# Spreading rotary tables, rotary key and row scales over partitions by DMA, and splitting the first weights of z one stage earlier

## The chip, the core and the metric

The kernel runs on one core of one Trainium2 chip. The metric is the device time of one execution in microseconds; a kernel's time is the median of its runs. TensorE does the matrix products, VectorE, ScalarE and GpSimd (POOL in the profile) the elementwise work, and DMAs are issued from the queues of SyncE (SP) and POOL.

## What is computed

One layer of an encoder: multi-head latent attention with a gate, then a gated embedding, on 1024 tokens of 1024 features in float32. The part that the change touches is the input side of the attention:

```python
h = rmsnorm(x, norm_g)
u = h @ w_in
c_q, c_kv, k_rope, z = split(u, [384, 640, 672])      # widths 384, 256, 32, 1024
q = (rmsnorm(c_q, q_norm) @ w_q_b)                    # 16 heads of 64 + 32
q_rope = apply_rope(q[..., 64:], cos, sin)
kv = (rmsnorm(c_kv, kv_norm) @ w_kv_b)                # 16 heads of 64 + 64
k_rope = apply_rope(k_rope, cos, sin)                 # one rotary key for all heads
...                                                   # scores, block-causal mask, softmax, values: o
y = (o * silu(z)) @ w_out
x = x + y
out = rmsnorm(x + sigmoid(rmsnorm(x) @ ple_gate) * (p @ ple_proj), final_norm)
```

## The kernel before

Every matrix product is made from float32 operands that are split into a high and a low part (`_hi`/`_lo`, `zh`/`zl`), and is the sum of three matmuls: hi*hi, hi*lo, lo*hi. A high part is a rounded copy, usually by ScalarE; the low part is the difference, usually by VectorE.

The stages on TensorE, one after the other, are: c_q, c_kv and the rotary key's input (`u_tile`, L203, eight tiles of 128 tokens, to 68.7 us); z (L487 to L509, eight products of 128 features by 1024 tokens, to 172 us); the projections of the first heads; then 16 heads of attention; then the output projection, the gate and the last norm.

In z each product c takes two half-products n = 2c and 2c + 1, of four 128x128 weight blocks each: 24 matmuls of 128x512 per half. `z_weights(n)` (L472) loads the half's weights to the staging tile `zs`, and splits them by four instructions on ScalarE (`zh`, L481) and four on VectorE (`zl`, L482). It is called one half-product ahead; there are three staging tiles and two pairs `zh`, `zl`, so a split waits until the half-product before last has been multiplied. These tiles lie where the weights of c_q, c_kv were, so no `zh`, `zl` can be written before that stage's last matmul. After a product VectorE multiplies it by `rbc`, the tokens' norm factors on all partitions (L498), which frees its PSUM tile (there are two, `ps_big`), and ScalarE makes the SiLU (L499).

Three things lie by token (token on the partition) and are needed by feature (token along the row): the norm factors `rx`, of which `rbc` has the same row on all 128 partitions; the rotary tables `cosT`, `sinT`, which become `cs`; and the rotary key `kr`, which becomes `kt` and then, split, half of `k_hi`, `k_lo` (L444 to L447). For each of them VectorE transposes 32x32 blocks and then places the blocks by 16 copies of 32 partitions each: `spread` (L449) for `rbc` and the two tables, `rope_key` (L426) for the key. `rope_key` stands in the text after product 1, the tables after product 2, the loads and casts of the first heads' weights (`weights(0)`, POOL, L381) after product 3, and the first rotary projections (`project_r`, which multiplies by `cs` and writes to DRAM from POOL's queue, L421) after products 4 and 5. Their scratch is two tiles of 4 KB per partition, `rt_tile` and `rh_tile`, of which there is one each.

The order of the text is not the order on an engine: the tile framework lists the instructions of each engine by its own estimate of when they are ready, the earlier text first among ready ones. On the chip each engine then runs its list strictly in order, and waits where an instruction's inputs are not there; DMA issues stand in the list of the engine whose queue they use.

Of the kernel before, what the change touches and what calls it, by code (L numbers as in the profile page):

```python
# [9 lines left out]
F32 = mybir.dt.float32  # L10
F32R = mybir.dt.float32r
BF16 = mybir.dt.bfloat16
I32 = mybir.dt.int32
AF = mybir.ActivationFunctionType
ALU = mybir.AluOpType
AX = mybir.AxisListType

P = 128
S = 1024
D = 1024  # L20
NT = S // P
KT = D // P
# [3 lines left out]
NOPE = 64  # L26
ROPE = 32
# [7 lines left out]
HF = ROPE // 2  # L35
# [16 lines left out]
def mla_ple_kernel(ctx, tc, x, x_t, p_t, pos, norm_g, w_c, w_z, q_norm, w_q, w_r, kv_norm, w_k, w_v,  # L52
# [6 lines left out]
    nc = tc.nc  # L59
    V, A, G = nc.vector, nc.scalar, nc.gpsimd  # L60
# [9 lines left out]
    def ps_tr():  # L70
        return psum.tile([P, 512], F32, tag="one", name="ps_tr", bufs=4)
# [8 lines left out]
    ident = const.tile([P, P], F32, name="ident")  # L80
# [4 lines left out]
    cosT = const.tile([P, NT, HF], F32, name="cosT")  # L85
    sinT = const.tile([P, NT, HF], F32, name="sinT")
    krw = const.tile([P, NT, ROPE], F32, name="krw")
    small = ctx.enter_context(pool("small", bufs=4))
# [4 lines left out]
    def rsqrt(v, n, name="rs_y", bufs=None):  # L93

        half = small.tile([P, n], I32, tag=f"rs_i{n}", name="rs_i", bufs=2)
        V.tensor_scalar(out=half, in0=v.bitcast(I32), scalar1=1, scalar2=None,  # L96
                        op0=ALU.logical_shift_right)
        y = small.tile([P, n], F32, tag=f"{name}{n}", name=name, bufs=bufs)
        V.tensor_scalar(out=y.bitcast(I32), in0=half, scalar1=-1, scalar2=0x5F3759DF,
                        op0=ALU.mult, op1=ALU.add)  # L100
        t = small.tile([P, n], F32, tag=f"rs_t{n}", name="rs_t", bufs=2)
        if n == 1:
            h = small.tile([P, 1], F32, tag="rs_h", name="rs_h", bufs=2)
            V.tensor_scalar(out=h, in0=v, scalar1=-0.5, scalar2=None, op0=ALU.mult)
            for _ in range(3):
                V.tensor_scalar(out=t, in0=y, scalar1=y, scalar2=h, op0=ALU.mult, op1=ALU.mult)  # L106
                V.scalar_tensor_tensor(out=y, in0=t, scalar=1.5, in1=y, op0=ALU.add, op1=ALU.mult)  # L107
            return y
        for _ in range(3):
            V.scalar_tensor_tensor(out=t, in0=y, scalar=-0.5, in1=y, op0=ALU.mult, op1=ALU.mult)  # L110
            V.tensor_tensor(out=t, in0=t, in1=v, op=ALU.mult)
            V.scalar_tensor_tensor(out=y, in0=t, scalar=1.5, in1=y, op0=ALU.add, op1=ALU.mult)
        return y
# [23 lines left out]
    def rt_tile(name):  # L137
        return both.tile([P, S], F32, tag="rt", name=name, bufs=1)

    def rh_tile(name):  # L140
        return both.tile([P, S], F32R, tag="rh", name=name, bufs=1)
# [4 lines left out]
    zT = zT_pool.tile([P, KT, S], F32, name="zT")  # L146
# [119 lines left out]
    def angles():  # L266
# [77 lines left out]
        V.scalar_tensor_tensor(out=cosT, in0=f, scalar=-2.0, in1=f, op0=ALU.mult, op1=ALU.mult)  # L344
        ts1(cosT, cosT, 1.0, ALU.add)

    pend = []
    for t in range(NT):
        un = u_tile(t)
        if t + 2 < NT:  # L350
            if t + 3 < NT:
                load_xT(t + 3)
            load_x(t + 2)
            stat_x(t + 2)
        if len(pend) == 2:
            u_transposes(*pend.pop(0))
        pend.append((t, un))
        if t == 4:
            angles()
        if t == NT - 2:  # L360
            mse = small.tile([P, NT], F32, name="mse", bufs=1)
            V.tensor_scalar(out=mse, in0=msx, scalar1=EPS, scalar2=None, op0=ALU.add)
            rx = rsqrt(mse, NT, name="rx", bufs=1)
    for t in range(NT):
        V.tensor_scalar(out=krw[:, t, :], in0=krw[:, t, :], scalar1=rx[:, t:t + 1], scalar2=None,
                        op0=ALU.mult)
# [40 lines left out]
    def project_r(g, hf):  # L407
# [12 lines left out]
        for z, d in zip((hi, lo), rq_of[g]):  # L420
            nc.gpsimd.dma_start(out=d.rearrange("c p n -> p c n")[:, :, cols], in_=z.bitcast(F32))  # L421

    def rope_key():  # L426
        kr = att1.tile([P, 512], F32, tag="ws", name="kr", bufs=2).rearrange("p (t n) -> p t n", t=NT)
        ra = small.tile([P, NT, HF], F32, name="ra", bufs=1)
        x1, x2 = krw[:, :, :HF], krw[:, :, HF:]
        k1, k2 = kr[:, :, :HF], kr[:, :, HF:ROPE]  # L430
        for dst, a, b, op in ((k1, cosT, sinT, ALU.subtract), (k2, sinT, cosT, ALU.add)):
            V.tensor_tensor(out=ra, in0=x2, in1=b, op=ALU.mult)
            V.tensor_tensor(out=dst, in0=x1, in1=a, op=ALU.mult)
            V.tensor_tensor(out=dst, in0=dst, in1=ra, op=op)
        V.tensor_copy(out=kr[:, :, ROPE:ROPE + HF], in_=k2)
        V.tensor_scalar(out=kr[:, :, ROPE + HF:], in0=k1, scalar1=-1.0, scalar2=None, op0=ALU.mult)
        blk, kt = rt_tile("kb"), rh_tile("kt").bitcast(F32)
        V.transpose(out=blk[:, :512], in_=kr.rearrange("p t n -> p (t n)"))
        b = blk[:, :512].rearrange("p (t f n) -> p f t n", t=NT, f=2)
        d = kt.rearrange("p (t q n) -> p q t n", q=4, n=32)  # L440
        for i in range(4):
            for j in range(4):
                V.tensor_copy(out=d[i * 32:(i + 1) * 32, j], in_=b[j * 32:(j + 1) * 32, i % 2])
        for e in range(2):  # L444
            rows = slice(NOPE * (1 - e), NOPE * (2 - e))
            A.copy(out=k_hi[e][rows], in_=kt[rows])
            sub_hi(V, k_lo[e][rows], kt[rows], k_hi[e][rows])  # L447

    def spread(src, dst, n):  # L449

        t, blk = rt_tile("spread"), rh_tile("blk").bitcast(F32)
        t, blk = (z[:, :NT * 32].rearrange("p (t n) -> p t n", t=NT) for z in (t, blk))
        V.tensor_copy(out=t.rearrange("p t (m n) -> p t m n", n=n) if n > 1 else t,
                      in_=src.unsqueeze(2).broadcast_to([P, NT, 32 // n, n]) if n > 1 else src.broadcast_to([P, NT, 32]))
        V.transpose(out=blk.rearrange("p t n -> p (t n)"), in_=t.rearrange("p t n -> p (t n)"))
        d = dst.rearrange("p (t q n) -> p q t n", q=4, n=32)
        for i in range(4):
            for j in range(4):
                V.tensor_copy(out=d[i * 32:(i + 1) * 32, j], in_=blk[j * 32:(j + 1) * 32])

    def rope_tables():
        for tab, src in zip(cs, (cosT, sinT)):
            spread(src, tab, HF)

    zph = ExitStack()

    zr = zph.enter_context(pool("zr", reuse_waits="tile"))
    rbc = zr.tile([P, S], F32, name="rbc")
    spread(rx.unsqueeze(2), rbc, 1)
    zw = zph.enter_context(pool("zw", reuse_waits="tile"))  # L470

    def z_weights(n):  # L472

        c, k0 = n // 2, n % 2 * 4
        stg, hi, lo = (zw.tile([P, 512], d, tag="z" + z, name="z" + z, bufs=m)
                       for z, d, m in (("s", F32, 3), ("h", F32R, 2), ("l", F32R, 2)))
        stg, hi, lo = (z.rearrange("p (k n) -> p k n", k=4) for z in (stg, hi, lo))
        nc.sync.dma_start(out=stg, in_=w_z[c].rearrange("p (k n) -> p k n", k=KT)[:, k0:k0 + 4, :])
        for k in range(4):
            g = g_col[:, k0 + k:k0 + k + 1]  # L480
            A.activation(out=hi[:, k, :], in_=stg[:, k, :], func=AF.Copy, scale=g)  # L481
            V.scalar_tensor_tensor(out=lo[:, k, :], in0=stg[:, k, :], scalar=g,  # L482
                                   in1=hi[:, k, :].bitcast(F32), op0=ALU.mult, op1=ALU.subtract)
        return hi, lo

    wz_next = z_weights(0)
    for c in range(KT):  # L487
        ps = ps_big()
        for k in range(KT):
            if k % 4 == 0:  # L490
                wz, n = wz_next, 2 * c + k // 4 + 1
                wz_next = z_weights(n) if n < 2 * KT else None
            for a, b in pairs:
                for hf in range(2):
                    nc.tensor.matmul(ps[:, hf * 512:(hf + 1) * 512], wz[b][:, k % 4, :],  # L495
                                     (hT_hi, hT_lo)[a][:, k, hf * 512:(hf + 1) * 512],
                                     start=k == 0 and a + b == 0, stop=k == KT - 1 and a == 1)
        V.tensor_tensor(out=zT[:, c, :], in0=ps, in1=rbc, op=ALU.mult)  # L498
        A.activation(out=zT[:, c, :], in_=zT[:, c, :], func=AF.Silu)  # L499
        if c < 2:  # L500
            u_transposes(*pend.pop(0))
        if c == 1:
            rope_key()
        if c == 2:
            rope_tables()
        if c == 3:
            weights(0)
        if c in (4, 5):
            project_r(0, c - 4)  # L509
# [157 lines left out]
    for n in range(len(blocks) + LAGV):  # L667
        if n < len(blocks):
            h, i = blocks[n]
# [208 lines left out]
```

## Time and profile before

| what | value |
|---|---|
| median of 3 runs | 728.67 us (726.36 to 729.4) |
| the profiled execution | 730.98 us |
| its span on the core | 729.2 us |
| TensorE busy | 708.6 us (97%) |
| VectorE busy | 547.4 us (75%) |
| ScalarE busy | 400.5 us (55%) |
| POOL busy | 198.8 us (27%) |

Matmuls are pipelined and their ends are modelled, so TensorE's busy share says only where it had something to do. Lost time in a stage is read from the starts of its matmuls, from the idle times and from the granted clock (1.00 is 2.4 GHz).

### The profile page before, as it was taken

Reading aid. Unit: us, or ns where it says so; the run is one execution under the profiler, and the core shown is the slowest. Engines: PE = TensorE matmul, PEld = TensorE weight load, DVE = VectorE, ACT = ScalarE, POOL = GpSimd, SP = SyncE. Lnnn points to the kernel's source line nnn. Section 1 sums busy time; section 2 is a strip of 40 time slices with the busy share of each in tenths; the row PEclk is TensorE's granted clock in tenths of the full one; section 3 lists DMA queues with packets and bytes.
Section 4 is the critical chain, followed back from the end, with each engine's and each line's share of the span. In section 5 each row is a group of like instructions: output and inputs, shape, how many; then the busy total and the mean of one; then the engine's idle time right before and its main releaser. Section 6 shows DMA issues by size and latency. Waiting matters only on the chain. (4 is left out here: it accounts for less than half of the span.)

```text
span 729.2 us, 11583 instructions
## 1 busy us (share of the span) xinstructions
PE 708.6 (97%) x4031; PEld 614.8 (84%) x4031; DVE 547.4 (75%) x1364; ACT 400.5 (55%) x919; POOL 198.8 (27%) x208
## 2 busy tenths in 40 slices
PE   9999989999999999999999999998999999999995
PEld 6998768888988999888999899887878887888884
DVE  6897894333988988888888888899654259798754
ACT  5743243334777786777768777776543144333322
POOL 0000300222225533453345532166146142000000
PEclk9999999999999999999999999999999999999998
DMA  8820311223102413034120431033474021111101
GB/s 305 286 86 1 105 40 48 79 95 95 51 16 82 141 30 88 15 106 129 45 75 0 152 99 45 16 113 91 136 283 130 1 82 35 44 36 37 58 29 58
DMA packets 25674, 61.32 MB, mean 84 GB/s; under 512 B 4112, under 2 KB 8080, under 8 KB 25616
## 3 DMA queue, kind: packets, MB, share of 16 engines
q1 hardware_dynamic: 23168, 52.19, 22.7%
q0 software_dynamic: 2304, 8.39, 3.1%
q8 instruction: 32, 0.52, 0.3%
q14 instruction: 26, 0.21, 0.1%
q10 hardware_dynamic: 144, 0.00, 0.0%
HBM read 47.92 MB, written 12.65 MB: 83 GB/s over the span
## 5 line engine op out<-in xcount | busy, mean ns | idle before, releaser
L733 PE MATMUL ps_big<-w,aTh 128*128 128x512 f32 (+1 forms) x480 | 139.1, 390 | 0.4 <-ACT sg L809 0.4
L733 PEld LDWEIGHTS ps_big<-w,aTh 128*128 128x128 f32 x480 | 89.4, 188 | 20.9 <-ACT sg L809 0.8
L601 ACT ACTIVATE prob<-ps_big,mx 128x384 f32<-128x384 f32 (+6 forms) x112 | 89.4, 799 | 16.3 <-DVE mx L596 15.7
L596 DVE TENSOR_REDUCE mx<-ps_big 128x1 f32<-128x384 f32 (+6 forms) x112 | 91.6, 817 | 1.8
L121 PE MATMUL ps_tr<-ident,prob 128*128 128x128 f32 x576 | 84.1, 273 | 1.9 <-ACT prob L601 1.9
L733 PE MATMUL ps_big<-w,aTl 128*128 128x512 f32 (+1 forms) x240 | 84.5, 390 | 0.1
L121 PEld LDWEIGHTS ps_tr<-ident,prob 128*128 128x128 f32 x576 | 68.3, 140 | 11.6 <-ACT prob L601 2.8
L91 DVE TENSOR_TENSOR pt8l<-ps_tr,pt8h 128x512 fp32r<-128x512 f32 (+3 forms) x128 | 71.0, 581 | 4.5 <-ACT pt8h L632 3.8
L591 PE MATMUL ps_big<-k_hi,qh 128*128 128x512 f32 (+2 forms) x176 | 67.7, 385 | 0.9 <-ACT prob L601 0.8
L649 POOL TENSOR_TENSOR zT<-o,zT 64x256 f32<-64x256 f32 x56 | 41.0, 734 | 94.8 <-DVE o L647 81.2
L632 ACT CAST pt8h<-ps_tr 128x512 fp32r<-128x512 f32 (+3 forms) x128 | 60.8, 509 | 4.7 <-PE ps_tr L121 4.3
L591 PE MATMUL ps_big<-k_lo,qh 128*128 128x512 f32 (+2 forms) x176 | 61.9, 352 | 0.0
L591 PE MATMUL ps_big<-k_hi,ql 128*128 128x512 f32 (+2 forms) x176 | 61.4, 349 | 0.0
L643 PE MATMUL ps_o<-pt8h,vals 128*128 128x256 f32 x224 | 57.6, 294 | 0.0
L643 PE MATMUL ps_o<-pt8l,vals 128*128 128x256 f32 x224 | 55.0, 282 | 0.0
L733 PEld LDWEIGHTS ps_big<-w,aTl 128*128 128x128 f32 x240 | 45.0, 188 | 10.2 <-POOL aTl L91 0.5
L495 PE MATMUL ps_big<-hT_hi,zh 128*128 128x512 f32 x128 | 41.3, 405 | 2.6 <-ACT zh L481 2.6
L481 ACT ACTIVATE zh<-zs,g_col 128x128 fp32r<-128x128 f32 x64 | 20.5, 397 | 42.4 <-PE ps_big L495 34.1
L495 PE MATMUL ps_big<-hT_hi,zl 128*128 128x512 f32 x128 | 40.7, 400 | 3.2 <-DVE zl L482 3.1
L116 ACT ACTIVATE jk<-xs 128x512 bf16<-128x512 f32 (+2 forms) x25 | 18.8, 750 | 44.9 <-DVE xs L811 37.0
L643 PEld LDWEIGHTS ps_o<-pt8l,vals 128*128 128x128 f32 x224 | 42.9, 191 | 0.0
L643 PEld LDWEIGHTS ps_o<-pt8h,vals 128*128 128x128 f32 x224 | 42.6, 190 | 0.0
(269 smaller groups left out, 1728.7 us busy)
## 6 DMA issues: line engine op xcount, KB each, us to landing
zT<-in_x SPq DMA_DIRECT2D x8, 512.0 KB, 4.8
zs<-in_w_z SPq DMA_DIRECT2D x16, 256.0 KB, 2.7
rlb<-rl SPq DMA_DIRECT2D x32, 128.0 KB, 3.1
wst<-in_w_out SPq DMA_DIRECT2D x8, 512.0 KB, 4.4
xs<-in_x SPq DMA_DIRECT2D x8, 512.0 KB, 7.4
wst<-in_ple_gate SPq DMA_DIRECT2D x8, 512.0 KB, 4.2
out<-xs SPq DMA_DIRECT2D x16, 256.0 KB, 2.0
zT<-in_x_t SPq DMA_DIRECT2D x6, 512.0 KB, 3.9
```

What stands on the lines that cost most here:

```text
L91: eng.tensor_tensor(out=lo, in0=src, in1=hi.bitcast(F32), op=ALU.subtract)
L116: A.activation(out=junk, in_=src, func=AF.Square, scale=n ** -0.5, accum_out=dst)
L121: nc.tensor.transpose(dst[:, j * P:(j + 1) * P], src[:, j * P:(j + 1) * P], ident)
L481: A.activation(out=hi[:, k, :], in_=stg[:, k, :], func=AF.Copy, scale=g)
L495: nc.tensor.matmul(ps[:, hf * 512:(hf + 1) * 512], wz[b][:, k % 4, :], (hT_hi, hT_lo)[a][:, k, hf * 512:(hf + 1) * 512], start=k == 0 and ...
L591: nc.tensor.matmul(ps[:, off + s0:off + s1], q[a][:, qs], (k_hi, k_lo)[b][e][:, s0:s1], start=a + b == 0, stop=a == 1)
L596: V.tensor_reduce(out=mx, in_=s, axis=AX.X, op=ALU.max, negate=True)
L601: A.activation(out=pr[:, :n], in_=s, func=AF.Exp, bias=mx, scale=1.0, accum_out=l)
L632: A.copy(out=hi[:, j0:j0 + n, half], in_=src)
L643: nc.tensor.matmul(ps[:, :256], w, z[:, j, :], start=j + n == 0, stop=j == last and n == 1)
L649: (V if h >= H - 2 else G).tensor_tensor(out=z, in0=o[top], in1=z, op=ALU.mult)
L733: nc.tensor.matmul(o, st[a][:, k, :], w[k][b][:, cols], start=k == 0 and a + b == 0, stop=k == nk - 1 and a == 1)
```

## The change

`rbc` is now made from a TensorE transpose of `rx`, written as a row of 4 KB to DRAM and read back to all 128 partitions by one DMA (`token_scales`). For the tables and the key, `token_rows` keeps VectorE's blockwise transposition, writes the blocks to a DRAM tile with one row per feature (four DMAs of 32 partitions for each 32 features, in runs of 128 bytes), and the rows are read back once for each place where they are needed: two reads for the key, four for each table. All these DMAs are issued from POOL's queue. The 16 copies of each are gone.

`z_weights` is moved ahead of the stage c_q, c_kv and called for half-products 0 and 1 in that stage's tile 6. These two are staged in `zT[:, 1, :]` and split into `rh_tile` and `rt_tile`. From then on weights are asked for two half-products ahead, with three pairs `zh`, `zl` and one staging tile.

```diff
@@ -344,6 +344,24 @@
         V.scalar_tensor_tensor(out=cosT, in0=f, scalar=-2.0, in1=f, op0=ALU.mult, op1=ALU.mult)
         ts1(cosT, cosT, 1.0, ALU.add)
 
+    def z_weights(n):
+
+        c, k0 = n // 2, n % 2 * 4
+        if n < 2:
+            cols = slice(n * 512, n * 512 + 512)
+            stg, hi, lo = (z[:, cols] for z in (zT[:, 1, :], *z_first))
+        else:
+            stg, hi, lo = (zw.tile([P, 512], d, tag="z" + z, name="z" + z, bufs=m)
+                           for z, d, m in (("s", F32, 1), ("h", F32R, 3), ("l", F32R, 3)))
+        stg, hi, lo = (z.rearrange("p (k n) -> p k n", k=4) for z in (stg, hi, lo))
+        nc.sync.dma_start(out=stg, in_=w_z[c].rearrange("p (k n) -> p k n", k=KT)[:, k0:k0 + 4, :])
+        for k in range(4):
+            g = g_col[:, k0 + k:k0 + k + 1]
+            A.activation(out=hi[:, k, :], in_=stg[:, k, :], func=AF.Copy, scale=g)
+            V.scalar_tensor_tensor(out=lo[:, k, :], in0=stg[:, k, :], scalar=g,
+                                   in1=hi[:, k, :].bitcast(F32), op0=ALU.mult, op1=ALU.subtract)
+        return hi, lo
+
     pend = []
     for t in range(NT):
         un = u_tile(t)
@@ -361,6 +379,8 @@
             mse = small.tile([P, NT], F32, name="mse", bufs=1)
             V.tensor_scalar(out=mse, in0=msx, scalar1=EPS, scalar2=None, op0=ALU.add)
             rx = rsqrt(mse, NT, name="rx", bufs=1)
+            z_first = rh_tile("z0h"), rt_tile("z0l").bitcast(F32R)
+            wz_of = {n: z_weights(n) for n in range(2)}
     for t in range(NT):
         V.tensor_scalar(out=krw[:, t, :], in0=krw[:, t, :], scalar1=rx[:, t:t + 1], scalar2=None,
                         op0=ALU.mult)
@@ -420,6 +440,18 @@
         for z, d in zip((hi, lo), rq_of[g]):
             nc.gpsimd.dma_start(out=d.rearrange("c p n -> p c n")[:, :, cols], in_=z.bitcast(F32))
 
+    def token_rows(name, src, n):
+
+        blk = rh_tile(name + "b").bitcast(F32)[:, :NT * n]
+        V.transpose(out=blk, in_=src.rearrange("p t n -> p (t n)"))
+        b = blk.rearrange("p (t f n) -> p f t n", t=NT, n=32)
+        d = tc.dram_tile([n, S], F32, name=name + "d")
+        for f in range(n // 32):
+            rows = d[f * 32:(f + 1) * 32, :].rearrange("r (t q n) -> q r t n", q=4, n=32)
+            for j in range(4):
+                nc.gpsimd.dma_start(out=rows[j], in_=b[j * 32:(j + 1) * 32, f])
+        return d
+
 
 
 
@@ -434,62 +466,48 @@
             V.tensor_tensor(out=dst, in0=dst, in1=ra, op=op)
         V.tensor_copy(out=kr[:, :, ROPE:ROPE + HF], in_=k2)
         V.tensor_scalar(out=kr[:, :, ROPE + HF:], in0=k1, scalar1=-1.0, scalar2=None, op0=ALU.mult)
-        blk, kt = rt_tile("kb"), rh_tile("kt").bitcast(F32)
-        V.transpose(out=blk[:, :512], in_=kr.rearrange("p t n -> p (t n)"))
-        b = blk[:, :512].rearrange("p (t f n) -> p f t n", t=NT, f=2)
-        d = kt.rearrange("p (t q n) -> p q t n", q=4, n=32)
-        for i in range(4):
-            for j in range(4):
-                V.tensor_copy(out=d[i * 32:(i + 1) * 32, j], in_=b[j * 32:(j + 1) * 32, i % 2])
+        kt = rt_tile("kt")
+        d = token_rows("kt", kr, 2 * ROPE)
+        for e in range(2):
+            nc.gpsimd.dma_start(out=kt[e * NOPE:(e + 1) * NOPE, :], in_=d)
         for e in range(2):
             rows = slice(NOPE * (1 - e), NOPE * (2 - e))
             A.copy(out=k_hi[e][rows], in_=kt[rows])
             sub_hi(V, k_lo[e][rows], kt[rows], k_hi[e][rows])
 
-    def spread(src, dst, n):
-
-        t, blk = rt_tile("spread"), rh_tile("blk").bitcast(F32)
-        t, blk = (z[:, :NT * 32].rearrange("p (t n) -> p t n", t=NT) for z in (t, blk))
-        V.tensor_copy(out=t.rearrange("p t (m n) -> p t m n", n=n) if n > 1 else t,
-                      in_=src.unsqueeze(2).broadcast_to([P, NT, 32 // n, n]) if n > 1 else src.broadcast_to([P, NT, 32]))
-        V.transpose(out=blk.rearrange("p t n -> p (t n)"), in_=t.rearrange("p t n -> p (t n)"))
-        d = dst.rearrange("p (t q n) -> p q t n", q=4, n=32)
-        for i in range(4):
-            for j in range(4):
-                V.tensor_copy(out=d[i * 32:(i + 1) * 32, j], in_=blk[j * 32:(j + 1) * 32])
-
     def rope_tables():
-        for tab, src in zip(cs, (cosT, sinT)):
-            spread(src, tab, HF)
+        for tab, src, name in zip(cs, (cosT, sinT), ("cos", "sin")):
+            t = rt_tile("spread")[:, :NT * 32].rearrange("p (t n) -> p t n", t=NT)
+            V.tensor_copy(out=t.rearrange("p t (m n) -> p t m n", n=HF),
+                          in_=src.unsqueeze(2).broadcast_to([P, NT, 32 // HF, HF]))
+            d = token_rows(name, t, ROPE)
+            for i in range(4):
+                nc.gpsimd.dma_start(out=tab[i * ROPE:(i + 1) * ROPE, :], in_=d)
+
+    def token_scales():
+
+        tr = ps_tr()
+        nc.tensor.transpose(tr[:NT, :P], rx, ident)
+        row = small.tile([2 * NT, P], F32, tag="row", name="row", bufs=1)[:NT]
+        A.copy(out=row, in_=tr[:NT, :P])
+        d = tc.dram_tile([S], F32, name="rxd")
+        nc.gpsimd.dma_start(out=d.rearrange("(t n) -> t n", n=P), in_=row)
+        nc.gpsimd.dma_start(out=rbc, in_=d.partition_broadcast(P))
 
     zph = ExitStack()
-
     zr = zph.enter_context(pool("zr", reuse_waits="tile"))
     rbc = zr.tile([P, S], F32, name="rbc")
-    spread(rx.unsqueeze(2), rbc, 1)
+    token_scales()
     zw = zph.enter_context(pool("zw", reuse_waits="tile"))
 
-    def z_weights(n):
-
-        c, k0 = n // 2, n % 2 * 4
-        stg, hi, lo = (zw.tile([P, 512], d, tag="z" + z, name="z" + z, bufs=m)
-                       for z, d, m in (("s", F32, 3), ("h", F32R, 2), ("l", F32R, 2)))
-        stg, hi, lo = (z.rearrange("p (k n) -> p k n", k=4) for z in (stg, hi, lo))
-        nc.sync.dma_start(out=stg, in_=w_z[c].rearrange("p (k n) -> p k n", k=KT)[:, k0:k0 + 4, :])
-        for k in range(4):
-            g = g_col[:, k0 + k:k0 + k + 1]
-            A.activation(out=hi[:, k, :], in_=stg[:, k, :], func=AF.Copy, scale=g)
-            V.scalar_tensor_tensor(out=lo[:, k, :], in0=stg[:, k, :], scalar=g,
-                                   in1=hi[:, k, :].bitcast(F32), op0=ALU.mult, op1=ALU.subtract)
-        return hi, lo
-
-    wz_next = z_weights(0)
     for c in range(KT):
         ps = ps_big()
         for k in range(KT):
             if k % 4 == 0:
-                wz, n = wz_next, 2 * c + k // 4 + 1
-                wz_next = z_weights(n) if n < 2 * KT else None
+                n = 2 * c + k // 4
+                wz = wz_of.pop(n)
+                if n + 2 < 2 * KT:
+                    wz_of[n + 2] = z_weights(n + 2)
             for a, b in pairs:
                 for hf in range(2):
                     nc.tensor.matmul(ps[:, hf * 512:(hf + 1) * 512], wz[b][:, k % 4, :],
```

## Rows read from the trace of the kernel before

**Rows 1.** The page, part 1: busy time, share and instructions.
```profile
PE 708.6 (97%) x4031; PEld 614.8 (84%) x4031; DVE 547.4 (75%) x1364; ACT 400.5 (55%) x919; POOL 198.8 (27%) x208
```

**Rows 2.** View of line L495: what PE and PEld sat idle for.
```profile
  DVE zl L482: 7.5, 5
  ACT zh L481: 5.9, 4
```

**Rows 3.** Windows: stretch, length, busy PE, PEld, DVE, ACT, POOL, clock, DMA share, GB/s.
```profile
61.27:68.74 7.47, 7.47 (x51) 7.47 (x50) 4.96 (x20) 1.47 (x7) 0.00 (x0) 1.00 0.00 0
68.74:77.43 8.69, 6.89 (x28) 5.22 (x27) 7.39 (x35) 4.66 (x17) 0.00 (x0) 0.80 0.15 51
...
89.70:92.94 3.24, 1.91 (x8) 0.97 (x6) 3.23 (x6) 3.19 (x6) 0.00 (x0) 1.00 0.17 40
...
103.56:111.75 8.19, 5.53 (x18) 4.09 (x17) 7.36 (x23) 2.52 (x6) 0.00 (x0) 0.79 0.10 32
...
161.35:172.23 10.88, 10.88 (x49) 9.01 (x48) 2.28 (x5) 2.27 (x5) 0.00 (x0) 1.00 0.00 1
```

**Rows 4.** Timeline of PE: start, length, instruction, [idle before, releaser].
```profile
68.74 1.25 PE L121 MATMUL ps_tr<-ident,zT 128*128 128x128 f32 x10
71.67 0.73 PE L495 MATMUL ps_big<-hT_hi,zh 128*128 128x512 f32 x2 [1.68 <-ACT zh L481]
...
97.52 0.71 PE L121 MATMUL ps_tr<-ident,zT 128*128 128x128 f32 x5
97.98 0.71 PE L495 MATMUL ps_big<-hT_hi,zh 128*128 128x512 f32 x2
...
106.83 0.72 PE L495 MATMUL ps_big<-hT_hi,zl 128*128 128x512 f32 x2 [2.66 <-DVE zl L482]
...
135.35 0.40 PE L403 MATMUL ps_pj<-cq_hi,wrh 128*128 128x512 f32 x1
...
137.44 0.62 PE L495 MATMUL ps_big<-hT_hi,zh 128*128 128x512 f32 x2
...
172.23 0.40 PE L535 MATMUL ps_pj<-ckv_hi,wkh 128*128 128x512 f32 x1
```

**Rows 5.** Timeline of ACT, the same columns.
```profile
89.71 1.04 ACT L446 CAST k_hi<-kt 64x1024 fp32r<-64x1024 f32 x1 [3.46 <-DVE kt L443]
...
105.75 1.06 ACT L499 ACTIVATE zT<-zT 128x1024 f32<-128x1024 f32 x1 [6.40 <-DVE zT L498]
```

**Rows 6.** Views of L459 and L443: ns min/median/max, first and last start.
```profile
L459 DVE COPY cs<-blk x32: 280/285/292, 95.2 to 109.7; 32x256 f32<-32x256 f32 x32
...
L443 DVE COPY kt<-kb x16: 274/285/1358, 82.8 to 88.3; 32x256 f32<-32x256 f32 x16
```

**Rows 7.** Timeline of DVE.
```profile
37.64 1.22 DVE L91 TENSOR_TENSOR hT_lo<-zT,hT_hi 128x1024 fp32r<-128x1024 f32 x1
...
77.54 0.71 DVE L438 STREAM_TRANSPOSE kb<-kr 128x512 f32<-128x512 f32 x1
...
156.59 1.23 DVE L482 SCALAR_TENSOR_TENSOR zl<-zs,g_col,zh 128x128 fp32r<-128x128 f32 x4 [4.57 <-ACT zh L481]
```

**Rows 8.** View of L478, the sixteen loads of `zs`.
```profile
DMA to landing us min/median/max: 2.6/2.7/8.4
```

**Rows 9.** Views of L481 and L482, the splits: ns min/median/max.
```profile
L481 ACT ACTIVATE zh<-zs,g_col x64: 384/388/460, 71.2 to 162.5; 128x128 fp32r<-128x128 f32 x64
...
L482 DVE SCALAR_TENSOR_TENSOR zl<-zs,g_col,zh x64: 333/346/1172, 72.1 to 163.5; 128x128 fp32r<-128x128 f32 x64
```

**Rows 10.** View of L421: issues on POOL's queue, ns min/median/max.
```profile
L421 POOL DMA_DIRECT2D rq0l<-rt x2: 727/729/731, 143.4 to 156.3; - x2
```

**Rows 11.** DMA view: issues, KB each, median us from issue to landing.
```profile
f_bc<-in_final_norm SPq DMA_DIRECT2D x1, 512.0 KB, 10.2
...
rq0l<-rt POOLq DMA_DIRECT2D x2, 512.0 KB, 4.8
...
rl<-row SPq DMA_DIRECT2D x8, 8.0 KB, 2.0
```

## The prediction

> **What bounds the kernel now.** I read the page's busy shares first: TensorE is busy for 97% of the span [rows 1], so time can come only from stretches in which it stands or runs slowly. The view of the line that issues z's matmuls (L495) names such a stretch: TensorE and its weight loads stood for 7.5 us until `zl` and 5.9 us until `zh` were there, the two halves of z's split weights [rows 2]. The stage windows say where, and what else was lost [rows 3]. From 61.27 to 68.74 us, the last tile of c_q, c_kv, TensorE has no gap, and none in z's last product from 161.35 to 172.23. In between three stretches have gaps, and in two of them the granted clock is 0.80 and 0.79 on average, where it is 1.00 elsewhere: between the levels of 2.4 and 1.2 GHz, and each time after TensorE had stood for 1.68 and 2.66 us [rows 4].
>
> How much is lost? z's eight products, 48 matmuls each, need 10.88 us each at full clock (161.35 to 172.23 [rows 3]): 87.0 us. Within the stage lie two rotary projections of 137.44 - 135.35 = 2.09 us [rows 4], and 15 transposes at 97.98 - 97.52 = 0.46 us for five [rows 4]. Needed: 87.0 + 4.2 + 1.4 = 92.6 us. Taken: 68.74 to 172.23, 103.5 us. So **10.9 us** are lost, and the rows give the places. Start: the ten transposes cover 0.92 us from 68.74, the first z matmul comes at 71.67, so 2.0 us of standing; then 5.76 us to 77.43 for eight pairs of matmuls, which take 10.88 / 24 = 0.453 each at full clock, so 2.1 us of slow clock. Half-product 3 (each half-product n is four of eight weight blocks): 3.24 us for three pairs from 89.70, 1.9 lost. Half-product 5: 8.19 us for eight pairs from 103.56, 4.6 lost, of it 2.66 of standing and 1.9 of slow clock. The rest is a few tenths.
>
> **Why it stands.** ScalarE's `zh` of n = 3 stood behind its copy of the rotary key, which had waited 3.46 us for `kt` [rows 5]; VectorE was writing `kt` in 16 copies, 285 ns in the median and up to 1358 ns [rows 6]. Around n = 5 ScalarE waited 6.40 us for VectorE's z evacuation [rows 5], which stood behind the 32 copies of cos and sin, 285 ns each [rows 6]. At the start nothing was split, because the split's buffers lie where the weights of c_q, c_kv had been.
>
> **The change, part by part.** *Copies of rows over partitions.* Gone from VectorE: in c_q, c_kv the 16 copies of `rbc`, of the tables' shape (16 x 0.285 = 4.6 us), in z the tables' 32 (9.1 us) and `kt`'s 16 (4.6 us by the median) [rows 6]. VectorE is late in z, so 13.7 us or more leave the engine that made n = 3 and n = 5 late.
>
> *First weights split early.* Half-products 0 and 1 go into buffers that are free after the load phase, staged in zT[:,1,:], which is free when the last `hT_lo` is made, 37.64 + 1.22 = 38.9 us [rows 7]. A 256 KB load of these weights lands in 2.7 us in the median [rows 8], so the splits can run from 42 us. They cost ScalarE 8 x 0.388 = 3.1 us and VectorE 8 x 0.346 = 2.8 us [rows 9]; VectorE gives back 4.6 us in the same stage, and ScalarE is busy for only 1.47 of 7.47 us there [rows 3]. So no TensorE time, cover about 27 us until they are wanted. If VectorE kept a PSUM tile too long, TensorE would stand; it had 2.5 us free in the last tile [rows 3]. Price 0, upper bound the 2.8 us.
>
> *Two half-products of lead.* Each split is asked for two half-products (10.9 us) ahead, with three pairs of buffers, and one staging buffer in place of three. With one, load and split take turns: landing 2.7 + four `zh` 1.55 + the last `zl` 0.35 = 4.6 us per half-product [rows 8, 9] against 5.44 needed. With one SiLU of 1.06 us [rows 5] per product: 10.3 against 10.88. Tight, but on the right side, and the lead covers single delays.
>
> *New DMAs on POOL's queue*, 28 issues: 2 for the row scales, 8 + 2 for the key, 4 + 4 for each table. A POOL issue takes 0.73 us [rows 10]. Scales: TensorE's tiny transpose (0.1 us) after c_q, c_kv at 69.2, ScalarE's copy near 71, the 4 KB write, 2.0 us by the nearest row [rows 11], an issue, then a 512 KB broadcast. The nearest rows for that are 2.7 us (a plain load of half the size [rows 8]) and 10.2 us (the one broadcast of this size, with the loads of x before it in its queue [rows 11]). So `rbc` is there between 78 and 85 us, and I count on 80; VectorE wants it at 80.2. Up to 5 us of VectorE waiting, with z's half-products 4 and later behind it; they aren't wanted before 91, and the PSUM tile is wanted back at 91. Price 0.
>
> Key: its buffer is shared with half-products 0 and 1, free at 69.3 + 10.9 = 80.2. The blockwise transposition, which both kernels make, takes 0.71 [rows 7]; the eighth write is issued 7 x 0.73 later, lands 2.0 (`rl`) to 4.8 us (`rq0l`, another write of POOL's queue) after that [rows 11]; of the two reads of 256 KB the second is issued 0.73 later and lands in 2.7 to 4.8: `kt` at 80.9 + 5.1 + 2.0 + 0.7 + 2.7 = 91.4 or at 96.3. The upper end is from POOL's own queue, so I take 96. Nobody on TensorE wants the key before the scores at 180 us. What can hurt is the queue: ScalarE's two copies of `kt` (1.04 us each [rows 5]) and VectorE's differences wait in order, and splits stand behind them. Tables follow the key on the same buffers; four issues, a landing, four issues, a landing make 10.5 to 15.4 us each, so after 98 they are back between 119 and 129. The first rotary projection's evacuation wants them at about 127; a miss of 2 us holds a PSUM tile of which there are four. Price 0, up to 2 us of VectorE.
>
> *The weights of the first heads* are cast on POOL, now among these issues, and wanted from 124.6 us on (69.3 + 5 x 10.88 + 0.9). By the trips above POOL is through with its issues by then at the latest, and between them it waits for landings; price 0, up to 4 us if all casts came last.
>
> **Sum.** Removable 10.9 us; I leave 0.5 us for the tiny transpose and small hand-overs: -10.4. The profiled execution takes 730.98 us (span 729.2), so 720.6; the median of the runs is 728.67, 2.3 below the profiled one, and the same difference gives **718.3 us**.
>
> **Rivals.** (1) *ScalarE's key copies stand ahead of n = 5's split.* For it: just this happened to n = 3 [rows 5]. n = 5 is wanted at 69.3 + 27.2 + 0.9 = 97.4. With `kt` at 96, copies 2.1, `zh` 1.55, `zl` 0.35: 100.0, a wait of 2.6 us, and, as with n = 5 before, 1.9 us of slow clock behind it: 4.5 lost, **722.8**. If the tables' buffers do it again, 9.0 lost: **727.3**. Against: three buffers let n = 4 be split before, and the engine can place the copies later.
>
> (2) *The same queue, with a slow trip: slower.* VectorE and POOL hold each other up in this trace: `kt`'s copies grew from 0.285 to 1.358 us beside POOL's work [rows 6]. If each of the key's ten issues grew by that 1.07 us, `kt` would land near 107, and n = 5 be split at 111.0: 13.6 us of standing and 1.9 of clock against the 10.4 gained: +5.1, **733.8**. The point from which it decides: `kt` landing after 102 us with ScalarE's copies ahead of n = 5. Against: POOL's issue at 156.30 ran beside VectorE's `zl` at 156.59 [rows 7] and took 0.73 as the other one did [rows 10], and the copies that were slow are what is taken away.
>
> The Trainium skill, "SBUF — State Buffer", section "SBUF: two separate sides", has a rule that speaks for (2): while VectorE runs an SBUF-to-SBUF operation in a two-port mode, GpSimd cannot write the descriptors of the DMAs it issues; the section "A bandwidth-pool intuition that's wrong (but worth ruling out)" gives about 620 ns alone and 3100 ns beside a copy. By that figure, an estimate, eight issues would last 25 us in place of 5.8, and the sum would be above rival 2's. The trace agrees for POOL's tensor operations and disagrees for its issues.
>
> (3) *One staging buffer paces z.* Loads landed in 2.6 to 8.4 us [rows 8]. Half-product n is ready at about 72 + (n - 2)(L + 1.9) for a landing of L and wanted, at n = 15, at 156: at L = 2.7 it is early by 24 us, at L = 5.0 late by 6 us, some 10 with slow clock in the proportion of n = 5: **728**.
>
> (4) *The early splits come late all the same*, by a buffer or a queue that I misjudge: the first 4.1 us stay, **722.4**.
>
> **Chances.** Forecast 0.60 (717 to 721); rival 1 0.17, twice over 0.06; rival 2 0.07; rival 3 0.05; rival 4 0.05. A measurement tells about 0.5% (3.6 us) from no change: below 725.0 faster, 0.60 + 0.17 + 0.05 = 0.82; within, 0.11; slower, 0.07. The range runs from 716.5 (all 10.9 us, and the 1 us by which runs differ) to 725.5, which holds forecast, rivals 1 and 4, and leaves out 2 in 10.
>
> **What will show it.** Right: z's first matmul within 1 us of 69.3; clock 1.00 through z; no standing at L495; the keys' projection starting near 162 in place of 172; everything behind it moved by the same amount. Wrong: idle time of L495 at n = 5 or later, ended by ScalarE or VectorE, whose own queue waits for a DMA of POOL (rivals 1, 2) or for `zs` (3); or gaps before 69 us.

## The result, and the profile after

The changed kernel takes 719.68 us (718.70 to 720.32), the kernel before 727.64 us beside it (726.36 to 729.40): ratio 0.9888, 95% interval 0.9860 to 0.9915, 8.0 us less. The forecast was 718.3 us, the range 716.5 to 725.5. The profiled execution takes 719.65 us with a span of 717.9; that of before took 730.98 with 729.2, so by the profiles the gain is 11.3 us.

The page's busy line of the changed kernel, to be held against [rows 1]:

```profile
PE 703.2 (98%) x4032; PEld 612.9 (85%) x4032; DVE 523.8 (73%) x1298; ACT 400.5 (56%) x920; POOL 214.2 (30%) x236
```

VectorE lost 66 instructions and 23.6 us of work, POOL gained 28 issues. None of that says where 11.3 us went; the timeline of TensorE does (start, length, instruction), beside [rows 4]. Where z's matmuls stood at L495 they now stand at L513:

```profile
68.19 0.71 PE L121 MATMUL ps_tr<-ident,zT 128*128 128x128 f32 x5
68.73 0.27 PE L490 MATMUL ps_tr<-ident,rx 128*8 128x128 f32 x1
68.76 0.70 PE L513 MATMUL ps_big<-hT_hi,z0h 128*128 128x512 f32 x2
```

z's first matmul follows the transposes at 68.76 us with no wait, where it was at 71.67. The windows (stretch, length, busy PE, PEld, DVE, ACT, POOL, clock, DMA share, GB/s): the start of z, the time of the last stretch that lost time in [rows 3], z's last product, then everything up to z, z itself, and everything behind it:

```profile
68.19:77.43 9.24, 9.24 (x46) 7.73 (x45) 7.26 (x33) 4.25 (x16) 2.84 (x4) 1.00 0.41 129
...
103.56:111.75 8.19, 8.19 (x38) 6.79 (x37) 2.52 (x6) 2.23 (x5) 6.30 (x12) 1.00 0.54 133
150.48:161.36 10.88, 10.88 (x49) 9.01 (x48) 1.23 (x1) 1.06 (x1) 0.00 (x0) 1.00 0.01 2
...
0.00:68.19 68.19, 66.42 (x419) 63.15 (x419) 53.35 (x229) 36.68 (x87) 1.24 (x22) 1.00 0.51 181
...
68.19:161.36 93.17, 93.17 (x420) 77.09 (x419) 39.02 (x103) 33.27 (x80) 29.41 (x42) 1.00 0.34 100
...
161.36:717.90 556.54, 543.59 (x3197) 472.71 (x3195) 431.45 (x966) 330.51 (x753) 183.54 (x172) 1.00 0.24 76
```

TensorE's busy time equals the length in every stretch of z, at clock 1.00. z with its transposes and rotary projections took 93.2 us; before it took 103.5, from 68.74 to 172.23 [rows 4]. That is 10.3 of the 11.3 us. Of the rest, 0.55 lies ahead of z (68.74 against 68.19) and 0.4 behind it (556.97 us from 172.23 to the span's end against 556.54). The first is within the scatter: the same transposes start at 68.40 in the second trace of the kernel before, and between 68.08 and 68.72 in the traces of the other kernels below.

What the two helping engines did around the key is the part that could have gone wrong. ScalarE's timeline, the last column the idle time before and its releaser, beside [rows 5]:

```profile
41.63 2.46 ACT L360 ACTIVATE z0h<-zT,g_col 128x128 fp32r<-128x128 f32 x8 [0.42 <-DMA zT<-in_w_z]
...
97.62 2.12 ACT L475 CAST k_hi<-kt 64x1024 fp32r<-64x1024 f32 x2 [2.25 <-DMA kt<-ktd]
99.77 1.28 ACT L360 ACTIVATE zh<-zs,g_col 128x128 fp32r<-128x128 f32 x4
106.17 1.28 ACT L360 ACTIVATE zh<-zs,g_col 128x128 fp32r<-128x128 f32 x4 [5.12 <-DMA zs<-in_w_z]
```

The splits of n = 0 and 1 ran at 41.63 us. Later ScalarE does wait for the key, and a split stands behind its copies: that of n = 7, at 99.77. Its `zl` follows at 101.21 and ends at 102.35, and n = 7's first matmul comes at 108.16: 5.8 us to spare. The least in the whole of z is 5.5 us, at n = 9 (113.57 and 119.04). POOL's timeline, beside [rows 10]:

```profile
70.53 0.71 POOL L494 DMA_DIRECT2D rxd<-row  x1 [68.72 <-ACT zh L360]
72.81 0.60 POOL L495 DMA_DIRECT2D rbc<-rxd  x1 [1.58 <-DVE rs_t L110]
...
83.18 0.47 POOL L401 CAST wkh<-ws 128x256 fp32r<-128x256 f32 x1 [2.15 <-DMA ws<-in_w_k]
83.73 0.74 POOL L91 TENSOR_TENSOR wkl<-ws,wkh 128x256 fp32r<-128x256 f32 x1
87.09 0.61 POOL L401 CAST wvh<-ws 128x512 fp32r<-128x512 f32 x1 [2.62 <-DMA ws<-in_w_v]
87.64 4.66 POOL L452 DMA_DIRECT2D ktd<-ktb  x8
...
94.21 1.07 POOL L472 DMA_DIRECT2D kt<-ktd  x2 [0.59 <-DMA ktd<-ktb]
...
114.80 1.98 POOL L485 DMA_DIRECT2D cs<-sind  x4 [2.96 <-DMA sind<-sinb]
```

### The profile page after: what moved, and what is told of

Its sections match the earlier page's. It is cut to its first block, busy times and chain, and to the rows that moved or that the text cites. A ratio compares the mean times of both kernels' runs of the same rounds, so it can differ in the third digit from the quotient of the medians.

```text
span 717.9 us, 11582 instructions
## 1 busy us (share of the span) xinstructions
PE 703.2 (98%) x4032; PEld 612.9 (85%) x4032; DVE 523.8 (73%) x1298; ACT 400.5 (56%) x920; POOL 214.2 (30%) x236
## 4 chain that ended last, share of the span: by engine, by line
PE 90%; DVE 3%; ACT 3%; DMA 2%; issue 1%; POOL 0%; SPq 0%; ACTq 0%; DVEq 0%
PE ps_big L751 21%; PE ps_big L609 13%; PE ps_big L513 12%; PE ps_o L661 10%; PE ps_tr L121 9%; PE ps_pj L423 6%; PE ps_big L215 4%; PE ps_pj L751 3%; PE ps_pj L570 3%; PE ps_pj L553 3%; PE ps_big L216 3%; PE ps_o L215 1%; PE ps_pj L216 1%; DMA wst<-in_w_out 1%; ACT prob L619 1%; PE ps_tr L609 1%
## 5 line engine op out<-in xcount | busy, mean ns | idle before, releaser
L751 PEld LDWEIGHTS ps_big<-w,aTl 128*128 128x128 f32 x240 | 45.0, 188 | 10.2 <-POOL aTl L91 0.5
L650 ACT CAST pt4h<-ps_tr 128x384 fp32r<-128x384 f32 (+3 forms) x64 | 27.2, 426 | 27.3 <-PE ps_tr L121 27.1
L360 ACT ACTIVATE zh<-zs,g_col 128x128 fp32r<-128x128 f32 x56 | 18.3, 392 | 42.1 <-DMA zs<-in_w_z 36.1
L609 PEld LDWEIGHTS ps_big<-k_hi,qh 128*128 128x128 f32 x176 | 33.2, 189 | 7.7 <-ACT prob L619 3.5
```

What stands on the lines that cost most here:

```text
L609: nc.tensor.matmul(ps[:, off + s0:off + s1], q[a][:, qs], (k_hi, k_lo)[b][e][:, s0:s1], start=a + b == 0, stop=a == 1)
L650: A.copy(out=hi[:, j0:j0 + n, half], in_=src)
L751: nc.tensor.matmul(o, st[a][:, k, :], w[k][b][:, cols], start=k == 0 and a + b == 0, stop=k == nk - 1 and a == 1)
```

## The experiments

All kernels below compute the full output; two of them copy the key more often than needed. "Ratio" is against the kernel before on the same chip (728.38 us for the first four, 728.86 for the others). The first four ran side by side, and so did the last four.

**The changed kernel once more**, for the scatter of its trace.

> The changed kernel itself, as the reference for the other runs on this chip. By the profile it should be about 11 us shorter than the kernel before in its span, and by the first timed runs about 8 us (ratio 0.989). If the profile's larger gain is real, the ratio is near 0.985; if the 8 us is, near 0.989. In z TensorE has no standing.

Measured: 719.53 us (719.23 to 720.64), ratio 0.9879 (0.9856 to 0.9902); profiled 719.23. The window from z's first matmul to the keys' projection:

```profile
69.04:161.64 92.60, 92.60 (x415) 76.54 (x413) 38.82 (x103) 33.01 (x80) 29.38 (x42) 1.00 0.33 101
```

What follows: z without a gap is no accident of one execution. The ratio lies near the 0.989 of the first timed runs and not near the 0.985 that the profiles give, so the smaller gain is the one that repeats. The profiled executions of this kernel lie within 0.3 us of the median of its runs, twice.

**The DMAs alone.** The weights are split as before: nothing early, one half-product ahead, three staging tiles, two pairs.

```diff
-            z_first = rh_tile("z0h"), rt_tile("z0l").bitcast(F32R)
-            wz_of = {n: z_weights(n) for n in range(2)}
...
+    wz_next = z_weights(0)
     for c in range(KT):
...
-                if n + 2 < 2 * KT:
-                    wz_of[n + 2] = z_weights(n + 2)
+                wz, n = wz_next, 2 * c + k // 4 + 1
+                wz_next = z_weights(n) if n < 2 * KT else None
```

> Only the first half of the change: rbc, the tables and the key go by DMA, but z's weights are split as before (nothing early, one half-product ahead, three staging tiles, two pairs). Theory A (VectorE's copies made n = 3 and n = 5 late): those two stalls are gone and only the start stays, 2.0 us of standing and 2.1 of slow clock, so a gain of 6.5 us in the profile (keys' projection starting near 165.5). Rival B (it is the second half-product of lead that helps, and with one the key's DMA trip takes the place of the copies, since ScalarE's key copies wait in order for it): stalls of 2 us or more stay at n = 3 to 7, gain below 3 us.

Measured: 722.51 us (721.50 to 723.20), ratio 0.9921 (0.9894 to 0.9948). TensorE's timeline at the start:

```profile
70.16 0.44 PE L121 MATMUL ps_tr<-ident,zT 128*128 128x128 f32 x2 [0.94 <-ACT row L472]
71.36 0.73 PE L506 MATMUL ps_big<-hT_hi,zh 128*128 128x512 f32 x2 [0.76 <-ACT zh L492]
```

Its windows of the first pairs and of the whole of z:

```profile
71.36:77.00 5.64, 5.64 (x25) 4.57 (x26) 5.54 (x27) 1.99 (x7) 0.60 (x1) 1.00 0.55 174
...
71.36:163.40 92.04, 92.04 (x408) 75.99 (x408) 39.55 (x102) 33.04 (x77) 29.93 (x41) 1.00 0.32 101
```

What follows: with VectorE's copies gone, z has no gap after its first matmul, though each half-product is split only one ahead. The start is still late, and that is what the other half of the change adds: 3.0 us in the runs, and in the traces 2.0 to the end of z (163.40 against 161.36). The end was expected near 165.5. The 2.1 us of slow clock counted on for the start did not come: the clock stayed at 1.00 behind 1.7 us of waiting in two parts.

**The early split and the lead of two alone.** VectorE's 64 copies are back.

```diff
-        kt = rt_tile("kt")
-        d = token_rows("kt", kr, 2 * ROPE)
+        blk, kt = rt_tile("kb"), rh_tile("kt").bitcast(F32)
...
+        for i in range(4):
+            for j in range(4):
+                V.tensor_copy(out=d[i * 32:(i + 1) * 32, j], in_=b[j * 32:(j + 1) * 32, i % 2])
...
-    token_scales()
+    spread_rx(rx.unsqueeze(2), rbc, 1)
```

> Only the second half of the change: half-products 0 and 1 split early, two half-products of lead, one staging tile; rbc, the tables and the key are spread by VectorE's copies as before (scratch of rbc's copies in zT). Theory A (the copies were the cause, and an engine that is behind stays behind): the start's 4.1 us come back, n = 5 or n = 6 still stalls by 3 us or more, gain 4 to 6 us. Rival B (the lead absorbs the copies): VectorE's list, summed from the rows of before, has n = 5's zl done at about 93.5 against 97.1 wanted, n = 6 at 100.7 against 102.7, n = 8 at 112.8 against 113.6: no stall over 1 us, gain as the whole change within 1 us. I hold B for likelier by this sum.

Measured: 720.04 us (719.62 to 720.50), ratio 0.9884 (0.9861 to 0.9906). The same window of z:

```profile
68.79:161.37 92.58, 92.58 (x416) 76.54 (x415) 56.30 (x151) 33.05 (x79) 14.13 (x14) 1.00 0.22 72
```

What follows: VectorE worked 56.3 us in z in place of 38.8, and TensorE did not stand for one of them. The DMAs are worth no time that these runs can tell beside the lead of two (720.04 against 719.53, intervals of the ratios almost the same). They are worth slack. VectorE's timeline ahead of n = 8, and n = 8's first matmuls on TensorE:

```profile
107.28 3.58 DVE L491 COPY cs<-blk 32x256 f32<-32x256 f32 x12
110.89 1.23 DVE L538 TENSOR_TENSOR zT<-ps_big,rbc 128x1024 f32<-128x1024 f32 x1
112.03 1.13 DVE L361 SCALAR_TENSOR_TENSOR zl<-zs,g_col,zh 128x128 fp32r<-128x128 f32 x4
...
113.60 0.62 PE L535 MATMUL ps_big<-hT_hi,zh 128*128 128x512 f32 x2
```

The split of n = 8 is done 0.45 us before its first matmul; in the changed kernel it is done 5.8 us before (107.84 and 113.60).

**The early split alone.** As the last, but one half-product ahead, with three staging tiles and two pairs.

```diff
-                           for z, d, m in (("s", F32, 1), ("h", F32R, 3), ("l", F32R, 3)))
+                           for z, d, m in (("s", F32, 3), ("h", F32R, 2), ("l", F32R, 2)))
...
-                if n + 2 < 2 * KT:
-                    wz_of[n + 2] = z_weights(n + 2)
+                if 1 < n + 1 < 2 * KT:
+                    wz_of[n + 1] = z_weights(n + 1)
```

> Half-products 0 and 1 split early and nothing else: copies by VectorE as before, one half-product of lead, three staging tiles, two pairs. The start's 4.1 us come back under every theory. TensorE then asks for n = 4 about 6 us earlier than before, while VectorE has the same copies: by the sum of its list n = 4 is late by 0.5 to 3 us and n = 5 by 1.5 to 2, each with slow clock behind it, so 4 to 8 of the 10.9 us stay lost: gain 3 to 7 us. If neither lead nor copies mattered, the gain would be the whole 10.9.

Measured: 722.67 us (720.91 to 723.77), ratio 0.9917 (0.9891 to 0.9944). TensorE's timeline at n = 5:

```profile
98.81 0.72 PE L535 MATMUL ps_big<-hT_hi,zl 128*128 128x512 f32 x2 [0.95 <-DVE zl L361]
```

The window behind that wait, and that of z:

```profile
98.81:104.25 5.44, 5.44 (x24) 4.42 (x24) 5.17 (x18) 1.55 (x6) 0.00 (x0) 1.00 0.15 48
...
68.75:163.01 94.26, 93.18 (x415) 76.38 (x413) 53.59 (x151) 33.15 (x79) 13.97 (x14) 1.00 0.20 65
```

What follows: with VectorE's copies and a lead of one, a wait for `zl` is there again, nearly all of it at n = 5, and costs z 94.26 - 92.60 = 1.7 us. It is smaller than the 2.66 us of [rows 4], and but for the place of a scratch tile the early split is all that differs from the kernel before. The clock stayed at 1.00.

**A slower trip of the key.** Three and seven DRAM-to-DRAM copies are put between the key's writes and its reads.

```diff
         d = token_rows("kt", kr, 2 * ROPE)
+        for j in range(3):
+            d, src = tc.dram_tile([2 * ROPE, S], F32, name=f"kt{j}x"), d
+            nc.gpsimd.dma_start(out=d, in_=src)
```

> The changed kernel with the key's way lengthened: three more copies of the key's 256 KB from DRAM to DRAM, one after the other on POOL's queue, before it is read back. From the rows after the change (issue 0.6, landing 3.7 us) each adds about 4.3 us, so the key lands near 110 us in place of 97.6. Rival 2 of the prediction had its deciding point at 102 us, if ScalarE's copies of the key stand ahead of a split that is wanted soon. In this kernel's ScalarE list they stand after half-product 7's split and the first quarter of 8's. Theory A (the lead pays for the wait): ScalarE goes on at 112.6, n = 8 is split by 114 and wanted from 113.6 on, so at most 1 us of standing, time as the changed kernel within 2 us. Rival B (a wait of ScalarE for POOL's DMA comes through to TensorE): 5 us or more lost.

Measured: 719.94 us (718.43 to 721.51), ratio 0.9877 (0.9852 to 0.9902). ScalarE's timeline:

```profile
108.88 1.05 ACT L478 CAST k_hi<-kt 64x1024 fp32r<-64x1024 f32 x1 [2.65 <-DMA kt<-kt2x]
110.67 1.04 ACT L478 CAST k_hi<-kt 64x1024 fp32r<-64x1024 f32 x1 [0.74 <-DMA kt<-kt2x]
111.75 1.28 ACT L360 ACTIVATE zh<-zs,g_col 128x128 fp32r<-128x128 f32 x4
```

The window of z:

```profile
68.92:161.53 92.61, 92.61 (x416) 76.55 (x413) 41.89 (x103) 32.94 (x80) 30.81 (x45) 1.00 0.36 109
```

What follows: the key came 11 us later and cost nothing. Each copy took 3.1 to 4.4 us from issue to issue. The split behind ScalarE's copies, at 111.75, was now by the count of splits that of n = 9, whose first matmul came at 119.2: the framework's list put the key's copies behind two more splits. With seven copies (the same diff with `range(7)`):

> As the run with three more copies, with seven: the key lands near 128 us, the tables, which follow on the same buffers, near 146 and 157, where the first rotary projection's evacuation wants them at 127. Theory A: z itself stays without standing over 1 us (n = 11 is ready at 131.8 and wanted at 132.0), but the first heads' rotary queries are written and read back only near 178 us, and the first scores, wanted near 170, wait 8 us: 725 to 730. Rival B (the waits stand ahead of splits on ScalarE and VectorE): standing in z at n = 11 to 15, 10 us or more.

Measured: 721.65 us (721.32 to 722.61), ratio 0.9903 (0.9884 to 0.9921). ScalarE's timeline, where the copies now stand ahead of n = 12:

```profile
121.57 2.12 ACT L478 CAST k_hi<-kt 64x1024 fp32r<-64x1024 f32 x2 [0.46 <-DMA kt<-kt6x]
```

The windows of z and of the first scores:

```profile
69.30:161.90 92.60, 92.60 (x416) 76.54 (x413) 38.92 (x103) 33.11 (x80) 32.04 (x48) 1.00 0.36 109
...
172.00:182.00 10.00, 9.23 (x61) 8.24 (x61) 8.36 (x20) 6.34 (x17) 1.05 (x1) 1.00 0.31 74
```

The second of these stretches in the changed kernel, as far behind the keys' projection:

```profile
171.46:181.46 10.00, 10.00 (x70) 9.32 (x69) 9.00 (x22) 6.66 (x19) 2.59 (x3) 1.00 0.07 25
```

What follows: z is untouched even by a key that is 24 us late. What the delay reaches is the tables behind it on POOL's queue: the last is back near 142 us, POOL writes the second half of the first rotary queries at 162.0 where the changed kernel writes it at 145.4, SyncE reads them at 165.8 in place of 162.9, and in the first scores TensorE has 61 matmuls in 10 us in place of 70. The cost in the runs, some 2 us, is far under what was expected, 725 to 730 us.

**Two staging tiles** in place of one.

```diff
-            stg, hi, lo = (zw.tile([P, 512], d, tag="z" + z, name="z" + z, bufs=m)
-                           for z, d, m in (("s", F32, 1), ("h", F32R, 3), ("l", F32R, 3)))
+            stg = zT[:, KT - 1, n % 2 * 512:n % 2 * 512 + 512]
+            hi, lo = (zw.tile([P, 512], d, tag="z" + z, name="z" + z, bufs=m)
+                      for z, d, m in (("h", F32R, 3), ("l", F32R, 3)))
```

> The changed kernel with two staging tiles in place of one for half-products 2 and later (they lie in zT[:, 7, :], which is written only by z's last product). Theory A: one staging tile is enough; ScalarE's 36 us of waiting for zs are slack, the closest split is 5.5 us early: time as the changed kernel within 1 us, and ScalarE's waits for zs become waits for the buffers of zh. Rival 3 of the prediction (staging paces z): 2 us or more faster.

Measured: 719.31 us (718.23 to 720.35), ratio 0.9863 (0.9842 to 0.9885), and the window of z:

```profile
68.81:161.41 92.60, 92.60 (x415) 76.56 (x413) 38.28 (x103) 33.18 (x80) 30.20 (x42) 1.00 0.34 104
```

What follows: a second staging tile changes nothing; one does not pace z.

**The kernel before once more**, to see whether its slow stretches come again.

> The kernel before, once more, for a second trace of it. The profiled execution shown lost 4.0 us to slow clock behind two waits (granted clock 0.80 and 0.79 there), while in the runs with only half of the change waits of 0.9 to 1.7 us left the clock at 1.00. Theory A: whether the clock falls behind such a wait differs from execution to execution, and that is why the kernels with waits spread by 2 to 4 us and those without by 1 to 2; this trace then either shows both dips and some 730 us, or fewer dips and 2 us less for each. Rival B: the dips come every time, and the runs' smaller gain (8 to 9 against 11.3 us) has another cause.

Measured: profiled 730.93 us; its runs on this chip had a median of 728.86. The two waits in TensorE's timeline:

```profile
71.33 0.73 PE L495 MATMUL ps_big<-hT_hi,zh 128*128 128x512 f32 x2 [1.68 <-ACT zh L481]
...
106.44 1.17 PE L495 MATMUL ps_big<-hT_hi,zl 128*128 128x512 f32 x2 [2.65 <-DVE zl L482]
```

The windows of [rows 3] in this trace:

```profile
68.74:77.43 8.69, 6.90 (x27) 5.18 (x26) 7.70 (x36) 4.55 (x17) 0.00 (x0) 0.80 0.20 64
103.56:111.75 8.19, 5.54 (x17) 4.26 (x17) 7.00 (x21) 2.52 (x6) 0.00 (x0) 0.79 0.10 32
```

What follows: waits and clock are those of the first trace, almost to the digit. In both profiled executions the kernel before loses the same.

## Why the prediction was right

**The place and the size of the loss** were right. Of the 10.9 us worked out for z, 10.4 were to come back; 10.3 did (93.2 against 103.5). The 92.6 us that the prediction said z needs are to be held against these 93.2, since both count all the transposes; that z takes 92.60 from its first matmul on is another count, without the first five. The keys' projection starts at 161.36, as "near 162" said.

**The last step of the sum was wrong**, by 1.4 us, inside the range. It took the 2.3 us between the profiled execution of before and the median of its runs over to the changed kernel. There the difference is nothing (719.65 against 719.68, 719.23 against 719.53), so the sum itself, 720.6, was the better forecast. In the gain the miss is larger: 10.4 us forecast, 8.0 measured (6.2 to 10.2 by the interval of the ratio). That the median of before came out at 727.64 in place of 728.67 made up 1.0 us of it, and that is luck.

Why the two profiled executions of before take 730.98 and 730.93 us, 2 to 3 us over its medians, is not shown. In the other kernels the profiled execution lies between 1.8 us under the median (the early split alone) and 1.0 over it (two staging tiles). It fits that two stretches of slow clock are priced at 2.1 + 1.9 us in the sum, and that kernels that wait less showed none. But the mean granted clock of an execution is on record for the runs too, and it speaks against this as the whole cause: the first profiled execution of before had 0.993, and three of its runs with the same 0.993 took 728.58 to 730.49 us. Single runs of before go from 726.36 to 731.14, so two profiled ones near 731 may in part be chance. This stays open.

**What made z late** was right, but its parts were not told apart. The prediction let VectorE's relief, the early split and the lead each do its share. The runs say: in the middle of z (n = 3 and 5) either half of the change is enough alone, the DMAs with a lead of one (no gap behind 71.36) or the lead of two with all of VectorE's copies (no gap at all). With neither, 1.7 us are lost even if the start is early. The early split together with the DMAs and a lead of one was not run, so no run here says whether the lead is needed beside them. The start belongs to the early split alone, and it is the only part without a substitute: 722.51 against 719.53. By these numbers the 64 copies that left VectorE are no gain of their own beside the lead; what they give is the slack, 5.8 us at n = 8 in place of 0.45.

**Rival 1** was half there: ScalarE's copies of the key did wait for a DMA and did hold a split, but that of n = 7, ready 5.8 us before its matmuls, and not that of n = 5. The term that failed is its place: the prediction took the order of before over, while the framework's list has these copies ahead of n = 7, 9 and 12 in the three kernels with 0, 3 and 7 more copies, behind more splits the longer the key's way. Nor did the place cost anything where it came about. With the DMAs alone ScalarE's copies of the key stood directly ahead of n = 5's split and did not wait for `kt`; ScalarE's timeline in that run:

```profile
89.28 2.10 ACT L455 CAST k_hi<-kt 64x1024 fp32r<-64x1024 f32 x2
93.49 0.69 ACT L492 ACTIVATE zh<-zs,g_col 128x128 fp32r<-128x128 f32 x2 [2.10 <-PE ps_big L506]
```

**Rival 2**'s deciding point, a key after 102 us with n = 5 behind it, did not come about: at 109 and at 121 us the key held only splits that were not wanted yet. Nor did POOL's issues grow by 1.07 us each; none of the eight lasted over 0.76. **Rival 3** fell with the second staging tile, **rival 4** with z's first matmul at 68.76.

**Single terms of the queue** were off in both directions. VectorE's transposition of the key came at 84.55 in place of 80.2, since it stood behind the split of n = 4. The eight issues began at 87.64, behind a cast of first-head weights that had waited 2.62 us for its load, a place in POOL's queue that the prediction had priced for the weights and not for the key. They took 4.66 us together, where eight times 0.73 make 5.8: each lasts 0.60 to 0.76 us, but the next one starts 0.54 to 0.61 us after it. ScalarE began its copies at 97.62, where `kt` was counted on at 96. `rbc` was issued at 72.81 and landed in 4.3 us, near 77 in place of 80; VectorE's first evacuation came at 81.12 without waiting for it. The last reads of the tables went out from 114.80 on and landed in 2.8 us, the last near 119, at the early end of 119 to 129. The range's lower end, 716.5, is 0.3 us under its own sum (728.67 - 10.9 - 1), which decided nothing.

VectorE's timeline in the changed kernel, beside POOL's cast and subtraction at 83.18 and beside those eight issues:

```profile
83.05 1.57 DVE L361 SCALAR_TENSOR_TENSOR zl<-zs,g_col,zh 128x128 fp32r<-128x128 f32 x3
...
88.40 1.23 DVE L361 SCALAR_TENSOR_TENSOR zl<-zs,g_col,zh 128x128 fp32r<-128x128 f32 x4 [3.16 <-ACT zh L360]
```

Beside POOL's issues four `zl` took 1.23 us, as they do at 121.12 with no work of POOL beside them, and the eight issues at 87.64 were not held up; beside POOL's cast and subtraction at 83.18 three of them took 1.57, the slowest 0.90 in place of 0.35. So here it is POOL's tensor operations that hold VectorE up, as the prediction read it; the 1.358 us of [rows 6] too stand beside a subtraction of POOL (from 88.24 to 89.53 us).

By the rule of the Trainium skill, "SBUF — State Buffer", section "SBUF: two separate sides", GpSimd cannot write the descriptors of its DMAs while VectorE runs an operation in a two-port mode; by the figure that the prediction took from the Trainium skill, these issues would then have been some 3 us each, an estimate. The prediction read the trace as disagreeing with the rule. That was too much, since the rows it used, like those of the changed kernel, have a two-input operation beside the issues. One copy of VectorE does fall wholly into an issue, in the kernel with seven more copies; VectorE's and POOL's timelines there:

```profile
126.97 0.28 DVE L484 COPY spread<-sinT 128x256 f32<-128x256 f32 x1
...
126.23 2.33 POOL L452 DMA_DIRECT2D cosd<-cosb  x4 [7.25 <-DVE cosb L446]
```

The copy took 0.28 us and the issue beside it 0.59, as elsewhere. Whether this copy runs in a two-port mode no run says, so the rule is neither shown nor refuted here.

## What to carry to other kernels

Price a stall by where TensorE's busy time falls short of a stretch's length, and add the slow clock behind it; for z that sum, less 0.5 us left for hand-overs, held to 0.1 us by the profiles. Where two parts of a change remove the same stall, run each alone before crediting either: here more lead hid work that the other part had gone to the trouble of removing, and only the slack ahead of each matmul told the two kernels apart. Don't carry a difference between the profiled execution and the median of the runs over to another kernel.

## What was not expected of the hardware

The new issues on POOL's queue lasted 0.49 to 0.76 us each, and their size says little: 0.49 to 0.52 for a copy of 256 KB inside DRAM, 0.60 for the broadcast of 512 KB, 0.60 to 0.76 for a 32 KB write in runs of 128 bytes, 0.71 for the 4 KB row. The 512 KB writes of [rows 10] had cost 0.73. A DRAM-to-DRAM copy of 256 KB landed in 2.8 to 3.8 us. The view of L452 in the changed kernel (ns min/median/max, first and last start):

```profile
L452 POOL DMA_DIRECT2D ktd<-ktb x8: 600/661/760, 87.6 to 91.5; - x8
```

A wait does not always cost clock. In both traces of before, waits of 1.68 and 2.65 us were followed by stretches at 0.80 and 0.79; with the DMAs alone, 0.94 and 0.76 us at nearly the same place, and with the early split alone, 0.95 us before a matmul, left it at 1.00, as did the two gaps between 89.70 and 92.94 in [rows 3]. The 0.80 and 0.79 are means over stretches with both levels. In the first trace the granted clock was 0.50, or 1.2 GHz, from 74 to 76 us and from 108 to 111, when TensorE had already resumed, at 71.67 and at 106.83.
